# Three feature blocks per tile at the change of token halves, token states reloaded in chunks of the contraction, and the mask conversion on GpSimd

## The chip, the cores and the metric

The kernel runs on one core of a Trainium2 chip. The metric is the device time of one execution in microseconds (us); three runs of the kernel before took 2374.8 to 2379.33 us, with a median of 2378.59 us.

## What is computed

A decoder block with two token mixers over 2048 tokens of width 1024. One projection of the normalised input feeds both. Branch A is dense causal attention with low-rank queries and keys (8 heads). Branch B is sparse: an indexer scores all visible keys for each query, 256 of them are kept, and only these are attended. Each branch has a gate, and two sigmoid gates merge the branches. Cut to the core:

```python
h = rms_norm(x, norm_gain[l]); proj = h @ w_in[l]
(c_q, c_kv, k_pe, gate_a, q_b, k_b, v_b, gate_b, q_i, k_i, w_i, m_a, m_b) = jnp.split(proj, offsets, axis=-1)
# indexer of branch B, for a block of 128 queries
rel = jax.nn.relu(jnp.einsum('bqhd,bsd->bqhs', q_i, k_i))
score = jnp.where(causal, jnp.einsum('bqhs,bqh->bqs', rel, w_i), -jnp.inf)
_, sel = lax.top_k(score, 256)
# after the two attentions o_a and o_b
merged = (jax.nn.sigmoid(m_a + b_merge[l, 0]) * ((o_a * jax.nn.silu(gate_a)) @ w_branch_mla[l])
          + jax.nn.sigmoid(m_b + b_merge[l, 1]) * ((o_b * jax.nn.silu(gate_b)) @ w_branch_dsa[l]))
x = x + merged @ w_out[l]
```

## The kernel before, in words

Matrix products that need float32 accuracy are split into a high and a low part and made of three products (`mm3`, lines 111 to 115). The kernel has four stages. The first (to about 345 us) normalises and transposes the tokens and projects them to the small pieces (`project_tokens`). The second (345 to about 1090 us, `project_features`) is the one that the change touches. The third holds the two attentions (to about 1900 us), the last the merge and the output projection.

**Feature blocks.** The gates are 24 columns of 128 features (`c`), computed for 4 groups of 512 tokens. SBUF holds the transposed token states of two groups at a time, `hT[0]` and `hT[1]`, each as a high and a low tile of 128 x 8 x 512 float32 (2.1 MB each). After the first stage these hold the second half of the tokens; the states of the first half were written to DRAM, one tensor `d_h[t]` per 128 tokens (line 228), and come back with `load_h` (lines 335 to 338): four DMAs of 128 tokens for each of the two tiles, 512 KB each. A block (`feat`, line 340) is one column for one group: 24 matmuls of 512 columns, 3 for each of 8 chunks of the contraction. `FEATURES` (line 1175) is the order of the blocks: mostly column by column, both groups in turn. At the change of halves the order is by group: the last two columns of the second half for group 0, then for group 1, then `load_h` has brought the first half, and the first two columns follow for group 0 and for group 1. `load_h(g)` is called after column 23 of group g (line 1109).

**Weights.** A column's weights take one of three buffers (`preload`, line 1082). The next column's load starts when the last block that uses the buffer is done. In the first pass a column is loaded from the input and split on GpSimd (lines 236 to 238, then 108 and 109); in the second pass the split weights come back from DRAM (`load_split`, line 1097).

**Beside the blocks.** Between groups of six feature matmuls ("slots") the same stage works off other lanes. The indexer (`index_pair`, `scores`) handles query tiles in pairs: a matmul per head and 512 keys into `z` (line 387, three PSUM banks), a Relu on ScalarE into `zr` (line 389, six buffers), and a multiply-add on VectorE into the score tile `sc` (line 392; the first head is a scaled copy on ScalarE, line 398). Score tiles have two buffers, so pair n+2 takes the buffer of pair n. The search (`search`, line 405) of pair n runs while pair n+1 is scored: five Sign passes on ScalarE (line 439) with small steps on VectorE, then scans on VectorE (MAX8 and MATCH_REPLACE8, lines 468 and 473). At its end the scores become a 0-or-large mask: a Relu with a bias on ScalarE, line 476, from `sc` to `bias` (one buffer), stored to DRAM by line 477. There are 7 pairs, so 14 conversions, of 384 to 2048 columns. The other lane (`prepare`, line 528) makes the queries and keys of branch A, with its normalisation on GpSimd (lines 88, 569 to 575).

**Order of work.** The order on TensorE is the program's own. On the other engines and the DMA queue of SyncE the framework orders the instructions by a simulated timeline; each engine then runs its own queue in that order, and a waiting instruction holds up all that stand behind it.

Of the kernel before, what the change touches and what calls it, by code (L numbers as in the profile page):

```python
# [9 lines left out]
F32 = mybir.dt.float32  # L10
# [4 lines left out]
AF = mybir.ActivationFunctionType  # L15
OP = mybir.AluOpType
# [4 lines left out]
P = 128  # L21
S = 2048
D = 1024
NT = S // P
NG = S // 512
KC = D // P
H = 8
NEG = -1.0e30
SELECTED = -4.0e30
# [38 lines left out]
def bcast(ap, n):  # L68
    return bass.AP(tensor=ap.tensor, offset=ap.offset, ap=[[0, P], [1, n]])


class Block:
# [55 lines left out]
    def setup(self):  # L128
        nc = self.nc
        cp = self.pool(self.ctx, "consts")  # L130
        self.dp = self.pool(self.ctx, "spill", space=DRAM)
        self.cp = cp
        self.front = ExitStack()
        self.back = ExitStack()
        bk = self.pool(self.front, "front")
        fr = self.pool(self.back, "back", side="right")
        self.gains = fr.tile([P, N_GAIN], F32, name="gains")
        self.bm = bk.tile([P, 16], F32, name="bm")
        self.guess = fr.tile([P, len(PAIRS), 2, 4], F32, name="guess")
        pos = fr.tile([P, NT], I32, name="pos")  # L140
        self.ident = cp.tile([P, P], F32, name="ident")
        self.identr = fr.tile([P, P], F32R, name="identr")
        self.identb = cp.tile([P, P], BF, name="identb")
        self.negb = cp.tile([P, P], BF, name="negb")
        self.shift = fr.tile([P, 1], F32, name="shift")
        self.tri = fr.tile([P, P], F32, name="tri")
        self.trib = cp.tile([P, P], BF, name="trib")
        self.ones = cp.tile([P, 64], F32, name="ones")
        self.iota8 = fr.tile([P, 8], F32, name="iota8")
        self.bad = cp.tile([P, 1], F32, name="bad")  # L150
        self.sel = fr.tile([P, 1], F32, name="sel")
        self.half = fr.tile([P, 1], F32, name="half")
        nc.vector.memset(self.half, -0.5)
        nc.vector.memset(self.ones, 1.0)
        nc.vector.memset(self.bad, 0.0)
        nc.vector.memset(self.sel, SELECTED)
        d = fr.tile([P, P], I32, name="diff")
        nc.gpsimd.iota(d, pattern=[[1, P]], base=0, channel_multiplier=-1)
        nc.vector.tensor_scalar(self.ident, d, 0.0, None, op0=OP.is_equal)
        nc.vector.tensor_scalar(self.identr, d, 0.0, None, op0=OP.is_equal)  # L160
        nc.vector.tensor_scalar(self.identb, d, 0.0, None, op0=OP.is_equal)
        nc.vector.tensor_scalar(self.negb, d, 0.0, -1.0, op0=OP.is_equal, op1=OP.mult)
        nc.vector.memset(self.shift, -SELECTED / 2)
        nc.vector.tensor_scalar(self.tri, d, 0.0, NEG, op0=OP.is_gt, op1=OP.mult)
        nc.vector.tensor_scalar(self.trib, d, 0.0, NEG, op0=OP.is_gt, op1=OP.mult)
        i8 = fr.tile([P, 8], I32, name="i8")
        nc.gpsimd.iota(i8, pattern=[[1, 8]], base=0, channel_multiplier=0)
        nc.vector.tensor_copy(self.iota8, i8)
        self.pos = pos
        self.cos = fr.tile([P, NT, 16], F32, name="cos")  # L170
        self.sin = fr.tile([P, NT, 16], F32, name="sin")
        self.hT = [[bk.tile([P, KC, 512], F32R, name="hT%d%s" % (g, s)) for s in "hl"] for g in range(2)]
        self.w_i = fr.tile([P, NT, H], F32, name="w_i")
        self.kpe = fr.tile([P, NT, 33], F32, name="kpe")
        self.kT = fr.tile([P, S], F32R, name="kT")
# [30 lines left out]
    def hidden(self, tok, t):  # L206
        nc = self.nc
        x = tok.tile([P, D], F32, name="x", tag="x", bufs=X_BUFS)
        nc.sync.dma_start(x, self.a["x"][t * P:(t + 1) * P, :])
        if t == 0:  # L210
            nc.sync.dma_start(self.gnorm, bcast(self.a["norm_gain"], D))
        junk = tok.tile([P, D], BF, name="xj", tag="xj")
        ssq = tok.tile([P, 1], F32, name="xs", tag="xs", bufs=2)
        nc.scalar.activation(junk, x, AF.Square, accum_out=ssq)
        rstd = self.rsqrt(tok, ssq, 1, 1.0 / D, "x")
        nc.vector.scalar_tensor_tensor(x, x, rstd, self.gnorm, op0=OP.mult, op1=OP.mult)
        yield
        i, sl = t % 8, slice(t % 4 * P, t % 4 * P + P)
        hi, lo = (m[:, :, sl] for m in self.hT[i // 4])
        for b in range(2):  # L220
            ps = self.pp.tile([P, 4, P], F32, name="tr", tag="tr", bufs=3)
            for k in range(4):
                kc = 4 * b + k
                nc.tensor.transpose(ps[:, k], x[:, kc * P:(kc + 1) * P], self.ident)
            self.split(nc.scalar, hi[:, 4 * b:4 * b + 4], lo[:, 4 * b:4 * b + 4], ps, eng_lo=nc.vector)
        if t < 8:
            for s, m in enumerate((hi, lo)):
                self.move(self.d_h[t][:, s], m)

    def load_w(self, pool, src, n, name, bufs, engines, stage=None):  # L230
        nc = self.nc
# [101 lines left out]


    def load_h(self, g):
        for i in range(4):
            for s in range(2):
                self.move(self.hT[g][s][:, :, i * P:(i + 1) * P], self.d_h[4 * g + i][:, s])

    def feat(self, ev, hf, g, c, w):  # L340
        nc = self.nc
# [63 lines left out]
    def search(self, ip, n, ts, scs):  # L405
        nc, v = self.nc, self.nc.vector
# [19 lines left out]
        nt, d = cur[:, :, 0:1], cur[:, :, 1:2]  # L426
# [30 lines left out]
        for i, (t, sc) in enumerate(zip(ts, scs)):  # L457
            W = sc.shape[1]
            m8 = ip.tile([P, S], U8, name="m8", tag="m8")[:, :W]
            v.tensor_scalar(m8, sc, th[:, i, 0:1], None, op0=OP.is_gt, op1=OP.add, accum_out=th[:, i, 1:2])  # L460
            yield
            v.copy_predicated(sc, m8, self.sel.to_broadcast([P, W]))
            yield
            for r in range(2):
                v8 = ip.tile([P, 8], F32, name="v8", tag="v8", bufs=2)
                pen = ip.tile([P, 8], F32, name="pen", tag="pen", bufs=2)
                need = ip.tile([P, 1], F32, name="need", tag="need", bufs=2)
                v.max(v8, sc)
                v.tensor_scalar(need, th[:, i, 1:2], -1.0, float(TOPK - 8 * r), op0=OP.mult, op1=OP.add)
                v.tensor_scalar(pen, self.iota8, need, 3.0e38, op0=OP.is_ge, op1=OP.mult)  # L470
                v.tensor_tensor(v8, v8, pen, op=OP.add)
                yield
                v.match_replace(sc, v8, sc, SELECTED)
                yield
            bias = ip.tile([P, S], BF, name="bias", tag="bias", bufs=1)[:, :W]
            nc.scalar.activation(bias, sc, AF.Relu, bias=self.shift)
            nc.sync.dma_start(self.d_m[t][:, :W], bias)
        v.tensor_scalar(th[:, :, 2:3], th[:, :, 1:2], -1.0, TARGET, op0=OP.mult, op1=OP.add)
        v.tensor_tensor(th[:, :, 2:3], th[:, :, 2:3], th[:, :, 2:3], op=OP.mult)
# [447 lines left out]
    def run(self):  # L927
        nc, a = self.nc, self.a
        self.setup()
        self.d_w = [self.dram([P, 2, KC, P], F32, "d_w%d" % m) for m in range(24)]  # L930
        self.d_h = [self.dram([P, 2, KC, P], F32, "d_h%d" % t) for t in range(NT // 2)]
        self.d_qi = [self.dram([P, H, 32], F32, "d_qi%d" % t) for t in range(NT)]
        self.d_c = [self.dram([P, 2, 3, P], F32, "d_c%d" % t) for t in range(NT)]
        self.d_qb = [self.dram([P, H, P], F32, "d_qb%d" % t) for t in range(NT)]
# [177 lines left out]
    def project_features(self, fp, ip, stream):  # L1112
# [23 lines left out]
        slots = 8 * (48 - TAIL)  # L1136
        period = (PREPARE_SPAN * slots - 16) / (NT + 0.5)
        lanes = [[index(), 0, 2 * 14 + 8 * 38, INDEX_FIRST, INDEX_SPAN * slots], [search(), 0, SEARCH_RATE * slots, 0, slots]]
        lanes += [[prepare(s), 0, (4 + PREPARE_GAP) * NT, 16 + period * s / 2, 16 + period * (s / 2 + NT)] for s in range(2)]
        for slot in range(1, slots + 1):  # L1140
# [34 lines left out]
def feature_order():  # L1175
    order = []
    for half in range(2):
        pairs = [(c,) for c in range(24)]
        pairs = pairs[:22] + [(22, 23)] if half == 0 else [(0, 1)] + pairs[2:]
        order += [(half, g, 24 * half + c) for p in pairs for g in range(2) for c in p]  # L1180
    return order


FEATURES = feature_order()


# [68 lines left out]
```

## Time and profile before

| | |
|---|---|
| median of three runs | 2378.59 us (2374.8 to 2379.33) |
| the profiled execution | 2380.04 us, with a span of 2378.1 us |
| mean granted TensorE clock | 0.986 of full speed |
| busy: PE, DVE, POOL, ACT | 95%, 59%, 50%, 42% of the span |
| HBM read and written | 184.2 MB and 139.3 MB |

PE is TensorE, DVE VectorE, ACT ScalarE, POOL GpSimd, SP SyncE (SPq its DMA queue). A row "A <- B: t, n" says that engine A sat idle t us in n places until B released it. In a timeline row the first number is the start in us from the span's start, the second the duration; brackets hold the idle time ahead of it and what ended it. PEclk is the granted clock; 1.00 is 2.4 GHz and the lower level is 1.2 GHz.

### The profile page before, as it was taken

How to read it: one execution, taken by the hardware profiler on the slowest of the kernel's cores; microseconds unless marked ns; L12 is line 12 of the kernel's file. 1: busy time of each engine (PE TensorE's matmuls, PEld its weight loads, DVE VectorE, ACT ScalarE, POOL GpSimd, SP SyncE). 2: the span in 40 equal slices, each digit the busy share in tenths (PEclk: the TensorE clock that was granted, in tenths of full speed). 3: DMA queues.
4: the chain of work that ended last, by engine and by line, in shares of the span. 5: the costliest groups of instructions: out<-in, count | busy, mean ns of one | idle time of the engine just before them, and what ended most of it. 6: DMA issues, size and time to landing. Idle time of an engine off the chain costs nothing. (4 is left out here: it accounts for less than half of the span.)

```text
span 2378.1 us, 37994 instructions
## 1 busy us (share of the span) xinstructions
PE 2267.0 (95%) x12882; PEld 1757.5 (74%) x12882; DVE 1414.3 (59%) x3296; ACT 996.4 (42%) x2002; POOL 1194.4 (50%) x1541
## 2 busy tenths in 40 slices
PE   6999989999998999999999999999999999999999
PEld 6999988777776878886565655655655557888888
DVE  6453525588686787756766676677778664222222
ACT  5342325666656668532434434434434443101110
POOL 5876958766653433412444434334855446433331
PEclk9999999999999999999999999999999999999999
DMA  9441355665659656667433421220313003444442
GB/s 306 142 146 53 117 164 173 226 214 184 230 179 268 210 155 192 200 203 220 126 100 104 125 63 45 77 75 28 114 48 92 24 15 119 145 135 134 126 125 84
DMA packets 298100, 326.12 MB, mean 137 GB/s; under 512 B 23408, under 2 KB 228592, under 8 KB 297776
## 3 DMA queue, kind: packets, MB, share of 16 engines
q1 hardware_dynamic: 297392, 323.56, 43.5%
q8 instruction: 101, 1.65, 0.3%
q14 instruction: 95, 0.78, 0.1%
q10 hardware_dynamic: 512, 0.13, 0.0%
HBM read 184.20 MB, written 139.26 MB: 136 GB/s over the span
## 5 line engine op out<-in xcount | busy, mean ns | idle before, releaser
L672 ACT ACTIVATE pt<-st 128x512 f32<-128x512 f32 (+3 forms) x640 | 340.3, 534 | 434.7 <-PE st L646 392.1
L679 POOL TENSOR_TENSOR acc<-acc,pt 128x512 f32<-128x512 f32 (+3 forms) x288 | 327.3, 1137 | 362.8 <-ACT pt L672 352.0
L392 DVE SCALAR_TENSOR_TENSOR sc<-zr,w_i,sc 128x512 f32<-128x512 f32 (+3 forms) x266 | 218.9, 826 | 109.7 <-ACT zr L389 105.4
L646 PE MATMUL st<-Q,K 96*128 96x512 f32 (+3 forms) x960 | 265.1, 383 | 0.5 <-ACT ev L352 0.5
L607 DVE CUSTOM_DVE_ANT_0 mj<-ap,mask 128x512 bf16<-128x512 f32 (+2 forms) x320 | 193.7, 605 | 102.8 <-PE ap L600 94.2
L604 DVE TENSOR_REDUCE mx<-ap 128x1 f32<-128x512 f32 (+2 forms) x320 | 185.2, 604 | 115.0 <-PE ap L600 66.0
L679 DVE TENSOR_TENSOR acc<-acc,pt 128x512 f32<-128x512 f32 (+3 forms) x288 | 218.6, 759 | 51.3 <-ACT pt L672 46.1
L646 PEld LDWEIGHTS st<-Q,K 96*128 96x128 f32 (+1 forms) x960 | 163.1, 191 | 72.5 <-issue 49.8
L389 ACT ACTIVATE zr<-z 128x512 f32<-128x512 f32 (+3 forms) x304 | 163.0, 545 | 93.6 <-PE z L387 89.1
L113 PE MATMUL acc<-hT1h,wfh 128*128 128x512 f32 x384 | 157.4, 410 | 8.0 <-DMA hT1h<-d_h 7.1
L113 PE MATMUL acc<-hT0h,wfh 128*128 128x512 f32 x384 | 155.0, 404 | 1.4 <-DMA hT0h<-d_h 1.2
L114 PE MATMUL acc<-hT1l,wfh 128*128 128x512 f32 x384 | 152.8, 398 | 1.4 <-DMA d_f<-ev 1.4
L115 PE MATMUL acc<-hT1h,wfl 128*128 128x512 f32 x384 | 152.7, 398 | 0.0
L114 PE MATMUL acc<-hT0l,wfh 128*128 128x512 f32 x384 | 151.2, 394 | 1.1 <-DMA hT0l<-d_h 1.1
L115 PE MATMUL acc<-hT0h,wfl 128*128 128x512 f32 x384 | 151.2, 394 | 0.0
L686 PE MATMUL o<-pt,Vb 128*64 128x512 f32 (+3 forms) x640 | 135.3, 544 | 0.0
L686 PE MATMUL o<-pt,V 128*64 128x512 f32 (+3 forms) x640 | 135.1, 543 | 0.0
L646 PE MATMUL st<-Q,Kd 128*128 128x512 f32 (+3 forms) x320 | 132.9, 416 | 0.0
L106 ACT ACTIVATE mh<-sg 128x256 fp32r<-128x256 f32 x64 | 26.7, 417 | 249.5 <-POOL sg L909 249.4
L907 DVE TENSOR_TENSOR sg<-br,sg 128x256 f32<-128x256 f32 x128 | 53.3, 423 | 129.9 <-PE br L115 68.0
L387 PE MATMUL z<-kT,iqT 128*128 128x512 f32 (+3 forms) x304 | 111.1, 369 | 14.5 <-ACT zr L389 14.4
L600 PE MATMUL ap<-Kd,Q 128*128 128x512 f32 (+2 forms) x320 | 115.0, 375 | 3.5 <-DVE mx L607 3.4
(283 smaller groups left out, 5974.9 us busy)
## 6 DMA issues: line engine op xcount, KB each, us to landing
d_f<-ev SPq DMA_DIRECT2D x96, 256.0 KB
sg<-d_f SPq DMA_DIRECT2D x128, 128.0 KB
wst<-in_w_f SPq DMA_DIRECT2D x96, 128.0 KB
d_w<-wfh SPq DMA_DIRECT2D x24, 512.0 KB
d_w<-wfl SPq DMA_DIRECT2D x24, 512.0 KB
d_q<-phl SPq DMA_DIRECT2D x32, 384.0 KB
d_k<-phl SPq DMA_DIRECT2D x32, 384.0 KB
wfh<-d_w SPq DMA_DIRECT2D x24, 512.0 KB
```

The costliest lines, as they stand in the source:

```text
L113: mm(ps, lhi, rhi, start=start, stop=False)
L114: mm(ps, lhi, rlo, start=False, stop=False)
L115: mm(ps, llo, rhi, start=False, stop=stop)
L389: nc.scalar.activation(r[:, :n], z[:, :n], AF.Relu)
L392: nc.vector.scalar_tensor_tensor(sc[:, k0:k0 + n], r[:, :n], ws, sc[:, k0:k0 + n], op0=OP.mult, op1=OP.add)
L600: nc.tensor.matmul(ps[:, :n], q[:, i * P:(i + 1) * P], k(b)[:, :n], start=True, stop=not diag)
L604: nc.vector.tensor_reduce(mx[:, b:b + 1], ps[:, :n], axis=AX, op=OP.max)
L607: nc.vector.tensor_tensor_reduce(out=junk[:, :n], in0=ps[:, :n], in1=mask[i][:, 512 * b:512 * b + n], scale=1.0, scalar=-3.0e38, op0=OP.su ...
L646: nc.tensor.matmul(banks[hh][:, cols], l, r, start=start and n == 0, stop=stop and n == len(seq) - 1)
L672: nc.scalar.activation(pt[:, n0:], ps[:, n0:], AF.Exp, scale=u["scale"])
L679: eng.tensor_tensor(acc[:, n0:], acc[:, n0:], pt[:, n0:], op=OP.add)
L686: self.nc.tensor.matmul(u["o"][64 * hh:64 * hh + 64, n0:], u["v"](hh, j), pts[hh][:, n0:], start=(j == 0), stop=(j == u["nk"] - 1))
```

## The change

It has three parts. At the change of halves three columns, not two, are done for group 0 before group 1, on both sides of the change. The token states of the first half are kept in one DRAM tensor per group, laid out like the SBUF tile, and come back in four DMAs of two contraction chunks (512 tokens wide) for each tile, still 512 KB each. The mask conversion is a `tensor_scalar` (add, then max with 0) on GpSimd, and the constant tile that held the bias goes.

```diff
-        self.shift = fr.tile([P, 1], F32, name="shift")
-        nc.vector.memset(self.shift, -SELECTED / 2)
...
         if t < 8:
             for s, m in enumerate((hi, lo)):
-                self.move(self.d_h[t][:, s], m)
+                self.move(self.d_h[t // 4][:, s, :, sl], m)
...
     def load_h(self, g):
-        for i in range(4):
+        for k in range(0, KC, 2):
             for s in range(2):
-                self.move(self.hT[g][s][:, :, i * P:(i + 1) * P], self.d_h[4 * g + i][:, s])
+                self.move(self.hT[g][s][:, k:k + 2], self.d_h[g][:, s, k:k + 2])
...
-            nc.scalar.activation(bias, sc, AF.Relu, bias=self.shift)
+            nc.gpsimd.tensor_scalar(bias, sc, -SELECTED / 2, 0.0, op0=OP.add, op1=OP.max)
             nc.sync.dma_start(self.d_m[t][:, :W], bias)
...
-        self.d_h = [self.dram([P, 2, KC, P], F32, "d_h%d" % t) for t in range(NT // 2)]
+        self.d_h = [self.dram([P, 2, KC, 512], F32, "d_h%d" % g) for g in range(2)]
...
-        pairs = pairs[:22] + [(22, 23)] if half == 0 else [(0, 1)] + pairs[2:]
+        pairs = pairs[:21] + [(21, 22, 23)] if half == 0 else [(0, 1, 2)] + pairs[3:]
```

## Rows read from the trace of the kernel before

**Rows 1.** The page: busy time, share and instructions of each engine.

```profile
PE 2267.0 (95%) x12882; PEld 1757.5 (74%) x12882; DVE 1414.3 (59%) x3296; ACT 996.4 (42%) x2002; POOL 1194.4 (50%) x1541
```

**Rows 2.** Waits of PE over the whole span: us in total, times, longest.

```profile
PE z L387 <- ACT zr L389: 14.4, 8, 3.4
...
PE acc L113 <- DMA hT1h<-d_h: 7.1, 1, 7.1
...
PE acc L114 <- DMA d_f<-ev: 1.4, 1, 1.4
...
PE acc L113 <- DMA hT0h<-d_h: 1.2, 1, 1.2
PE acc L114 <- DMA hT0l<-d_h: 1.1, 1, 1.1
```

**Rows 3.** Windows, long: length, busy PE, PEld, DVE, ACT, POOL, PEclk, DMA, GB/s.

```profile
690.00:780.00 90.00, 74.72 (x336) 61.53 (x336) 56.60 (x125) 55.91 (x106) 29.46 (x30) 0.91 0.82 249
780.00:1085.00 305.00, 301.46 (x1428) 249.71 (x1427) 219.58 (x474) 184.28 (x339) 104.40 (x104) 0.99 0.62 192
```

**Rows 4.** Timeline of PE at the change of halves.

```profile
727.95 0.28 PE L387 MATMUL z<-kT,iqT 128*128 128x256 f32 x1
...
731.33 0.39 PE L115 MATMUL acc<-hT0h,wfl 128*128 128x512 f32 x1
...
746.70 0.39 PE L387 MATMUL z<-kT,iqT 128*128 128x512 f32 x1
754.24 0.76 PE L113 MATMUL acc<-hT1h,wfh 128*128 128x512 f32 x1 [7.15 <-DMA hT1h<-d_h]
...
761.01 0.40 PE L115 MATMUL acc<-hT1h,wfl 128*128 128x512 f32 x1
```

**Rows 5.** Timeline of the SP queue: first issue of each of the two reloads.

```profile
713.41 0.37 SPq L121 DMA_DIRECT2D hT0l<-d_h  x1
...
733.52 0.81 SPq L121 DMA_DIRECT2D hT1h<-d_h  x1
```

**Rows 6.** DMA issues in 713:731, and the window in which the second reload lands.

```profile
hT0l<-d_h SPq DMA_DIRECT2D x4, 512.0 KB
```

```profile
749.00:755.00 6.00, 0.76 (x1) 0.29 (x1) 4.64 (x10) 1.54 (x4) 5.68 (x5) 0.63 1.08 296
```

**Rows 7.** What the mask conversion waits for, and two of the 14 in ACT's timeline.

```profile
  DVE sc L473: 23.8, 10
```

```profile
517.11 2.00 ACT L476 ACTIVATE bias<-sc,shift 128x2048 bf16<-128x2048 f32 x1 [4.95 <-DVE sc L473]
...
887.76 1.57 ACT L476 ACTIVATE bias<-sc,shift 128x1536 bf16<-128x1536 f32 x1 [6.87 <-DVE sc L473]
```

**Rows 8.** Timeline of PE: three waits for `z` right behind conversions.

```profile
519.65 0.80 PE L387 MATMUL z<-kT,iqT 128*128 128x512 f32 x1 [3.37 <-ACT zr L389]
...
691.54 0.33 PE L387 MATMUL z<-kT,iqT 128*128 128x128 f32 x1 [1.53 <-ACT zr L389]
...
889.88 0.50 PE L387 MATMUL z<-kT,iqT 128*128 128x512 f32 x1 [3.33 <-ACT zr L389]
```

**Rows 9.** Windows of 10 us around two of them.

```profile
505.00:515.00 10.00, 10.00 (x47) 8.21 (x46) 10.00 (x18) 5.40 (x10) 10.00 (x13) 1.00 0.28 90
515.00:525.00 10.00, 6.63 (x21) 5.15 (x20) 9.44 (x17) 5.37 (x8) 5.77 (x6) 0.67 0.96 347
885.00:895.00 10.00, 6.67 (x23) 5.00 (x22) 10.00 (x18) 6.83 (x11) 2.47 (x4) 0.83 0.46 167
895.00:905.00 10.00, 10.00 (x46) 8.27 (x45) 7.69 (x16) 7.11 (x16) 6.98 (x7) 1.00 0.79 232
```

**Rows 10.** POOL: a one-input operation of 512 columns, and a wait in its timeline.

```profile
L677 POOL TENSOR_SCALAR acc<-pt x64: 618/621/632, 1092.7 to 1950.3; 128x512 f32<-128x512 f32 x64
```

```profile
896.85 0.68 POOL L88 TENSOR_SCALAR rs_p<-pss 128x8 f32<-128x8 f32 x1 [9.30 <-DVE pss L565]
```

**Rows 11.** ACT's first write into the reused score tile, and POOL's split of column 23.

```profile
529.01 0.72 ACT L398 ACTIVATE sc<-zr,w_i 128x512 f32<-128x512 f32 x1
```

```profile
684.74 0.67 POOL L108 TENSOR_SCALAR wfh<-wst 128x256 fp32r<-128x256 f32 x1 [4.31 <-DMA wst<-in_w_f]
```

**Rows 12.** The multiply-add of the scores on DVE: ns min, median, max.

```profile
L392 DVE SCALAR_TENSOR_TENSOR sc<-zr,w_i,sc x266: 334/750/2159, 360.9 to 1008.5; 128x512 f32<-128x512 f32 x100, 128x384 f32<-128x384 f32 x15, 128x256 f32<-128x256 f32 x10, 128x128 f32<-128x128 f32 x8
```

## The prediction, made before the changed kernel was run

> **What bounds the kernel now.** I read the page first: PE is busy 2267.0 of 2378.1 us [rows 1], so the kernel goes as fast as PE is fed, and only PE's 111 us of idle time, and the time it runs at its lower clock, can be won without removing products. The change removes no product. Next I read the list of PE's waits. Two families touch the change [rows 2]: 14.4 us of waiting for a `z` bank that ACT has not emptied, and 7.1 + 1.4 + 1.2 + 1.1 = 10.8 us of waiting for reloaded token states (the 1.4 is put down to a store, but the product reads hT1's low part and stands right behind the 7.1). Then the long windows, to see where this falls: 15.3 us are idle between 690 and 780 at a clock of 0.91, but only 3.5 in the 305 us behind it [rows 3]. Last the timelines, because a stall costs more than its idle time: after one, PE runs some products at half clock.
>
> **Part 1, the change of halves.** Undisturbed, a product of 512 columns starts every 0.23 us, one of 256 every 0.12 us (half of it is my estimate). The first reload makes the third product behind the `z` at 727.95 start at 731.33 [rows 4]; undisturbed it would be 727.95 + 0.12 + 2 x 0.23 = 728.53. Loss 2.8 us. In the second, 13 products start from 746.70 up to 761.01; at 0.23 they take 3.0 us, they took 14.3. Loss 11.3 us, though the waits are only 7.1 + 1.4: the rest is the low clock. Together **14.1 us** is all that part 1 can win.
>
> What must be true for that? The first reload is issued at 713.41 and needed at 727.95, 14.5 us of cover by two blocks, 7.3 us each [rows 4, 5]. It moves 8 x 512 KB = 4.2 MB; at the 296 GB/s of a window full of such traffic that is 14.2 us [rows 6], so it just misses. With three blocks the cover is about 21.8 us. The second reload is wanted from 727.95, but SP issues it only at 733.52, 5.6 us later, with the first reload's weights and stores ahead of it; PE comes for it at 746.9, after 18.9 us, of which 2.8 are the first stall, and gets it at 754.2. So it lands 26.3 us after it could have been issued, with 16.1 us of work as cover. Three blocks give 24.1 us at 8 us each. Pessimistically (nothing gets faster) 2.2 us of stall remain, some 4 us with the clock. But the 26.3 us include queueing behind the first reload, whose last piece had only just landed; with a block more between the two reloads its 14.2 us are over before the second begins: 5.6 us of issue delay, 3.5 us for one column's weights (1.05 MB at 296 GB/s) and 14.2 us make 23.3 us. And the pieces are now chunks of the contraction: a block's first six products need only the first chunk pair, the last pair is needed some 5 us later, whereas each token piece was needed by the first product. The new pieces are also longer runs in both memories; I give no gain for that, the cover suffices without it. So 10 to 14 us, and I take **-13 us**.
>
> What the move costs: the eight stores of each layout in the first stage are the same in number and bytes, and I take nothing for them; the SBUF side keeps its 512-byte runs. A store is issued with x loads behind it on SP's queue, so bounds are 0 and +1 us. Column 23's weights are now wanted two blocks after their buffer is free instead of three, and each of columns 24 to 27 two blocks ahead instead of three or four. Column 23 is split on POOL: its last piece starts at 684.74 [rows 11] and ends about 1.5 us later. The new order reaches column 23 for group 0 two blocks ahead of 713.41 [rows 5]; with a stall among them [rows 8] that is 691 to 699. Cover at least 5 us; if a conversion stands ahead of the piece in POOL's queue (the one in front of 691.54), it comes at about 693 to 694, and the last chunk pair is read some 5 us into the block. Bounds 0 and +3 us, taken as 0. The second-pass weights need no POOL, 3.5 us of transfer against 15 us of cover.
>
> **Part 2, the conversion.** On ACT it costs more than its time: ACT stands still for 23.8 us in 10 places until the last scan on DVE is done [rows 7], and everything behind it waits too, the Relu that empties `z` among it. The three waits in [rows 8] stand right behind conversions: at 517.11 ACT had been idle 4.95 us and then worked 2.00; at 887.76 it was 6.87 and 1.57 [rows 7]. Their price by the windows: 21 products where the window before has 47 is 26/47 of 10 us, 5.5 us; 23 against 46 in the window after is 5.0 us [rows 9]. With 1.5 us for the small one, **12.0 us**. The other waits for ACT in that family come behind Sign passes of the search, which stay.
>
> What the conversion costs on POOL: 14 of them, 17,024 columns together. A one-input operation of 512 columns takes 0.62 us there [rows 10], 1.2 ns a column, so some 21 us, 2.5 us for the longest. Cover: POOL is busy 104 of the last 305 us [rows 3], and at the conversion of 887.76 it sat idle for 9.30 us up to 896.85 [rows 10]. The waiting moves with it: POOL now stands until the scan is done, and behind it stand a weight split or the normalisation of `prepare`, which is asked for 17 slots, some 30 us, later. What is late next: DVE's own scans hold up the multiply-adds, but six `zr` buffers lie between them and PE. ACT's first write into the reused score tile waits for the conversions of two pairs back; the tightest is at 529.01 [rows 11], and POOL would end the second conversion at about 526 to 527, so 2 us of cover are left; without them ACT would stall there for the difference. Bounds for the whole part: all 12 us won, or none of it, since the framework orders four queues anew and a Sign pass can stand where the conversion stood. I take **-10 us**, near the upper end, because the idle row of POOL at the very place is the nearest one.
>
> **Sum.** 2380.04 (span 2378.1 plus 1.9 around it) - 13 - 10 = 2357.0 us. The profiled execution stands 1.45 us above the median shown, so against that I predict 2356 us, 1.0% less.
>
> **A rule against the change.** While POOL works, the multiply-add on DVE takes up to 2.16 us instead of its median 0.75 [rows 12], and in the windows where searches end DVE is already busy 10.0 and 9.4 of 10 us [rows 9]. The Trainium skill (GPSIMD Engine Reference, Specifications and Engine selection) says that GpSimd shares its SBUF interface with VectorE and contends with VectorE instructions that have two SBUF inputs, and advises VectorE for elementwise work, though one-input operations are near line rate; the spread of that row agrees with the contention. By it alone the second part would cost, not gain; it is the last rival below.
>
> **Rivals.** *Only the reload pays.* The search still stops ACT at its Sign passes, and the queues are ordered anew, so waits for `z` come back elsewhere for the same sum. For it: ACT's waits are between two engines that both run near a limit here. Against: three stalls stand directly at the conversions. Time: 2378.6 - 13 = 2366 us.
> *Weights take the place of tokens.* With three buffers and three columns per group, each column has two blocks of cover in place of four; a late split of column 23 and a weight load behind a reload cost 3 us idle each, 5 with the clock, as in the windows above. Time: 2356 + 10 = 2366 us. Against: 3.5 us of transfer each.
> *No change.* One part wins and the other loses about as much: 2378 us.
> *Slower: contention at the end of each search.* The place is DVE between the last scans and the next multiply-adds. During a conversion of some 1.5 us on average (21 us in 14) a multiply-add takes 1.4 us longer, and the following small steps too; if DVE falls more than six `zr` buffers behind, PE stops, and a stall of 1.3 us idle with its low clock costs about 2.6. It decides if it happens at nearly every conversion: 14 x 2.6 = 36 us less the 23 gained gives 2391 us. Against it: PE did not stop at most of the 14 places while ACT was stopped too.
>
> **How the numbers follow.** A difference under 0.2%, 4.8 us, is about what a measurement of this kernel can't tell from none. Forecast with both parts, 2346 (all of both, and the ordering kind) to 2361: 0.60. Only the reload, 2361 to 2370: 0.19. Late weights, same times: 0.08. No change: 0.06. Slower: 0.07. The range 2346 to 2370 holds the first three, 0.87, less what may fall beyond either end. Faster 0.87, same 0.06, slower 0.07.
>
> **What would show it.** Right: no wait of PE for a reload above 1 us, and a clock near 1.00 between 690 and 780; no ACT idle time in front of a conversion, and POOL idle instead until the same scan; the wait for `z` down from 14.4 to 4 to 6 us. Wrong: a wait of PE on weights around columns 23 to 27; a scaled copy on ACT waiting for POOL; longer multiply-adds on DVE with waits for `z` at the same places; a wait for `z` as large as before, now behind Sign passes.

## The result and the profile after

The changed kernel takes 2404.88 us (median of four runs, 2398.43 to 2407.56) against 2378.11 of the kernel before in the same series (2374.80 to 2379.33): ratio 1.0102, 95% interval 1.008 to 1.0124. It is slower by 1%. The forecast was 2356 us, 1% faster, with 2346 to 2370 as its range. Of the two parts one did what was forecast: no reload of token states is left in PE's list of waits, and PE is better fed at the change of halves. The other lost more than the first won.

The profiled execution took 2402.92 us, its span 2400.9. The page's busy row; DVE is busy 21.6 us and POOL 62.3 us longer than in [rows 1], ACT 19.3 us shorter:

```profile
PE 2277.5 (95%) x12882; PEld 1764.5 (73%) x12882; DVE 1435.9 (60%) x3295; ACT 977.1 (41%) x1988; POOL 1256.7 (52%) x1555
```

PE's waits over the whole span (us in total, times, longest), to be held against [rows 2]:

```profile
PE tr L581 <- DVE phl L109: 16.2, 2, 9.2
...
PE z L385 <- ACT zr L387: 11.0, 8, 3.0
PE tr L581 <- ACT iqT L376: 7.3, 2, 6.6
...
PE acc L113 <- ACT pqk L558: 6.0, 3, 3.3
PE tr L118 <- DVE phl L109: 3.9, 1, 3.9
```

The wait for `z` fell from 14.4 to 11.0 only. In place of the reload stand waits of up to 9.2 us for work of `prepare` (`phl`, `pqk`) and of the index (`iqT`), which DVE and ACT deliver late. The long windows show where the time went (length, busy PE with its products, PEld, DVE, ACT, POOL, granted clock, DMA share, GB/s):

```profile
345.00:690.00 345.00, 324.31 (x1494) 266.42 (x1495) 245.30 (x439) 209.91 (x405) 260.04 (x313) 0.98 0.58 194
690.00:780.00 90.00, 78.28 (x367) 65.08 (x366) 61.78 (x130) 53.67 (x107) 46.91 (x40) 0.94 0.75 260
780.00:1085.00 305.00, 289.23 (x1332) 239.64 (x1331) 223.91 (x450) 173.63 (x328) 132.58 (x106) 0.97 0.55 176
```

The first of these windows in the kernel before:

```profile
345.00:690.00 345.00, 329.73 (x1526) 271.94 (x1525) 244.81 (x456) 217.19 (x412) 244.07 (x309) 0.98 0.61 201
```

Between 690 and 780 PE starts 367 products in place of the 336 of [rows 3]. It starts 32 fewer in the window ahead and 96 fewer in the one behind (1332 in place of 1428). At the forecast's 0.23 us each, an estimate since some products are shorter, 128 products lost and 31 gained make 22 us; the span grew by 22.8. POOL is busy 132.6 us in the last window, not 104.4.

**The conversion on POOL.** First the line's own row (count, min, median, max in ns), then some of the 14 in the list of groups by shape (busy us, mean ns, idle before):

```profile
L474 POOL TENSOR_SCALAR bias<-sc x14: 1501/4310/7100, 519.7 to 1078.5; 128x2048 bf16<-128x2048 f32 x1, 128x384 bf16<-128x384 f32 x1, 128x1920 bf16<-128x1920 f32 x1, 128x512 bf16<-128x512 f32 x1
```

```profile
L474 POOL TENSOR_SCALAR bias<-sc 128x2048 bf16<-128x2048 f32 x1 | 7.1, 7100 | 3.6 <-DVE sc L471 3.6
...
L474 POOL TENSOR_SCALAR bias<-sc 128x1152 bf16<-128x1152 f32 x1 | 4.1, 4092 | 6.2 <-DMA d_f<-ev 6.2
...
L474 POOL TENSOR_SCALAR bias<-sc 128x512 bf16<-128x512 f32 x1 | 1.9, 1927 | 0.1
```

That is 3.5 ns a column, where the forecast had 1.2 from [rows 10]; the 14 sum to 61.9 us, not 21, and the longest takes 7.1 us, not 2.5. The one of 1152 columns ran at 1078.53, when DVE had nothing to do, and took 3.55 ns a column all the same: the price is the instruction's own.

**What it does to DVE.** The timeline of POOL, then DVE, at the first conversion:

```profile
519.68 7.10 POOL L474 TENSOR_SCALAR bias<-sc 128x2048 bf16<-128x2048 f32 x1 [3.64 <-DVE sc L471]
...
520.31 0.54 DVE L471 MATCH_REPLACE8 sc<-v,sc 128x384 f32<-128x384 f32 x1
520.77 3.44 DVE L480 TENSOR_TENSOR bad<-bad,th 128x1 f32<-128x1 f32 x1
524.12 0.74 DVE L390 SCALAR_TENSOR_TENSOR sc<-zr,w_i,sc 128x512 f32<-128x512 f32 x1
524.79 2.02 DVE L563 TENSOR_SCALAR pss<-pss,kpe 128x8 f32<-128x8 f32 x1
```

The same steps in the kernel before:

```profile
517.79 0.54 DVE L473 MATCH_REPLACE8 sc<-v,sc 128x384 f32<-128x384 f32 x1
518.25 0.14 DVE L482 TENSOR_TENSOR bad<-bad,th 128x1 f32<-128x1 f32 x1
518.32 0.74 DVE L392 SCALAR_TENSOR_TENSOR sc<-zr,w_i,sc 128x512 f32<-128x512 f32 x1
518.98 0.22 DVE L565 TENSOR_SCALAR pss<-pss,kpe 128x8 f32<-128x8 f32 x1
```

A scan goes on undisturbed beside POOL (0.54 us both times), but an operation on a single column, with two inputs, takes 3.44 us in place of 0.14, and a small one with a value per partition 2.02 in place of 0.22. DVE works in order, so the multiply-adds of the scores stand behind them. The Trainium skill (SBUF — State Buffer, "Who interferes with whom") says that a VectorE instruction with two SBUF inputs contends with a GpSimd instruction that reads SBUF. By the 3.44 us against 0.14 this trace agrees. The same section says of VectorE's modes with two ports that whoever comes first holds the shared ports for the whole instruction, and that the other is blocked, not slowed. The one-column operation was not held so long: it ended at 524.21, while the conversion ran until 526.78.

**How it reaches PE.** Two of the stalls, first ACT and PE after the conversion just shown, then DVE and PE after the one of 1792 columns that started at 701.55 (the last number in brackets is the idle time before, with what ended it):

```profile
530.83 0.52 ACT L412 ACTIVATE junk<-sc 128x384 bf16<-128x384 f32 x1 [10.34 <-DVE sc L390]
...
531.98 1.09 PE L581 MATMUL tr<-ident,pqk 128*96 128x128 f32 x4 [6.57 <-ACT iqT L376]
...
701.77 5.02 DVE L390 SCALAR_TENSOR_TENSOR sc<-zr,w_i,sc 128x512 f32<-128x512 f32 x2
...
710.10 0.68 DVE L109 TENSOR_TENSOR phl<-tr,phl 96x512 fp32r<-96x512 f32 x1
710.83 1.09 PE L581 MATMUL tr<-ident,pqk 128*96 128x128 f32 x4 [9.16 <-DVE phl L109]
```

At the first, ACT no longer stands at the conversion; it stands 10.34 us at the next search's first statistics pass, which needs the last multiply-add of the scores, and `iqT` is queued behind that pass. At the second, two multiply-adds that take 0.75 us each by their median take 5.02 us together, `phl` comes behind them, and PE stops for 9.16 us. The longest single multiply-add is now 4.66 us; in [rows 12] it was 2.16.

### The profile page after: what moved, and what is told of

Its sections match the earlier page's. It is cut to its first block, busy times and chain, and to the rows that moved or that the text cites. A ratio compares the mean times of both kernels' runs of the same rounds, so it can differ in the third digit from the quotient of the medians.

```text
span 2400.9 us, 38042 instructions
## 1 busy us (share of the span) xinstructions
PE 2277.5 (95%) x12882; PEld 1764.5 (73%) x12882; DVE 1435.9 (60%) x3295; ACT 977.1 (41%) x1988; POOL 1256.7 (52%) x1555
## 4 chain that ended last, share of the span: by engine, by line
PE 54%; DVE 13%; DMA 6%; issue 5%; ACT 5%; POOL 4%; SPq 1%; DVEq 0%; ACTq 0%; POOLq 0%
PE st L644 17%; PE o L684 11%; PE ap L598 5%; DVE sc L390 4%; PE acc L113 3%; PE acc L114 3%; PE acc L115 3%; ACT junk L437 2%; DMA out_dram<-mx 2%; PE br L113 2%; PE br L115 2%; PE br L114 2%; PE ou L115 2%; PE ou L114 2%; PE ou L113 2%
## 5 line engine op out<-in xcount | busy, mean ns | idle before, releaser
L390 DVE SCALAR_TENSOR_TENSOR sc<-zr,w_i,sc 128x512 f32<-128x512 f32 (+3 forms) x266 | 225.1, 849 | 99.2 <-ACT zr L387 94.8
```

Source lines behind the costliest of these rows:

```text
L390: nc.vector.scalar_tensor_tensor(sc[:, k0:k0 + n], r[:, :n], ws, sc[:, k0:k0 + n], op0=OP.mult, op1=OP.add)
```

## The experiments

Two theories to begin with. **T**: only the conversion on GpSimd was mispriced, and it makes the whole loss. **R1**: the new order of blocks and queues makes the new stalls, whatever engine converts.

**1. The reload's part alone** (the change, with the conversion as before):

```diff
-            nc.gpsimd.tensor_scalar(bias, sc, -SELECTED / 2, 0.0, op0=OP.add, op1=OP.max)
+            nc.scalar.activation(bias, sc, AF.Relu, bias=self.shift)
```

> The change with its conversion put back on ACT: three blocks per tile and the reload by chunks alone. T (the conversion on GpSimd was mispriced and makes the whole loss, the reload pays as forecast): 2362 to 2369 us, against 2378 of before, and no wait of PE on the token states in its list. R1 (the new order of the blocks and queues makes the new stalls of PE, whatever engine converts): 2378 us or more, with PE's waits on the weights' and the index's values (7 to 9 us each) still there.

Measured: 2362.34 us against 2381.08 of before on that chip, ratio 0.9916 (0.9894 to 0.9939). In its list of waits no wait for a reloaded token state is left. T holds, R1 falls. The windows:

```profile
345.00:690.00 345.00, 326.88 (x1526) 269.54 (x1524) 244.50 (x458) 217.99 (x414) 244.21 (x310) 0.99 0.61 200
690.00:780.00 90.00, 85.54 (x404) 72.02 (x405) 62.73 (x133) 61.52 (x118) 33.92 (x33) 0.96 0.79 272
780.00:1085.00 305.00, 301.01 (x1424) 246.97 (x1425) 218.96 (x487) 180.80 (x333) 103.35 (x103) 0.99 0.63 197
```

Sixty-eight products more than in [rows 3] between 690 and 780, with nearly the same number as before on either side (1526 and 1428 there): the gain sits at the change of halves.

**2. The conversion's part alone** (the kernel before, with line 476 in the change's form):

> The kernel before with only the conversion moved to GpSimd. T: 2410 to 2420 us, the 14 conversions 55 to 65 us in all on POOL, and PE waits of 7 us or more behind late first passes of the next search. R1: 2366 to 2382 us, since the order of the blocks is that of before.

Measured: 2412.24 us, ratio 1.0128 (1.0111 to 1.0145). By itself the second part costs some 30 us. In the change it costs 36 to 44 us by the ratios (1.0102 against 0.9916 of the reload alone, and against 0.9949 in its second series, under 6); the intervals leave open whether the two parts simply add. Its 14 conversions take as long as in the change (1502 to 7100 ns), and PE's waits for `phl` (8.7 us the longest) and `iqT` (6.6) are there in the old order of blocks too.

**3. The conversion on DVE:**

```diff
-            nc.gpsimd.tensor_scalar(bias, sc, -SELECTED / 2, 0.0, op0=OP.add, op1=OP.max)
+            nc.vector.tensor_scalar(bias, sc, -SELECTED, None, op0=OP.add)
```

> The change with the conversion as one subtraction on DVE (the chosen values become 0, the others 4e30 instead of 2e30, so the mask is the same). T: it costs DVE what its other passes over f32 cost, some 14 to 20 us in all and nobody waits behind it on POOL: 2358 to 2372 us. If DVE at the end of a search is itself what the next search and PE wait for, 2372 to 2390 us. R1: above 2395 us, since the order stays.

Measured: 2375.19 us, ratio 0.9974 (0.9958 to 0.9989). The 14 conversions cost DVE 12.7 us, on an engine that the search itself waits for; the result lies in the second of the three ranges, 13 us above the reload alone on the same chip.

**4. What makes a column cost 3.5 ns?** Two forms by turns:

```diff
-            nc.gpsimd.tensor_scalar(bias, sc, -SELECTED / 2, 0.0, op0=OP.add, op1=OP.max)
+            if n % 2:
+                nc.gpsimd.tensor_scalar(bias, sc, 1.0, -SELECTED, op0=OP.mult, op1=OP.add)
+            else:
+                nc.gpsimd.tensor_scalar(sc, sc, -SELECTED / 2, 0.0, op0=OP.add, op1=OP.max)
+                nc.scalar.activation(bias, sc, AF.Copy)
```

> The change with two other forms of the conversion by turns. Odd pairs: multiply by 1 and add on GpSimd, from f32 to bf16. Even pairs: add and maximum on GpSimd from f32 to f32 in place, and then a copy to bf16 on ACT. It is meant to tell which feature makes a column cost 3 to 4 ns instead of the 1.2 ns of the forecast. If the bf16 output does: even pairs 1.2 ns, odd pairs 3 to 4 ns a column. If the operations do (the maximum): even pairs 3 to 4 ns, odd 1.2. If the place and its neighbours on DVE do: both 3 to 4 ns, the one that runs alone at the end less. Time of the whole: 2390 to 2415 us by any of the three.

```profile
L477 POOL TENSOR_SCALAR sc<-sc 128x1536 f32<-128x1536 f32 x1 | 5.4, 5393 | 2.4 <-DVE sc L471 2.4
...
L475 POOL TENSOR_SCALAR bias<-sc 128x1920 bf16<-128x1920 f32 x1 | 1.8, 1794 | 1.1 <-DVE sc L471 1.1
```

Add and maximum cost 3.5 ns a column with an f32 output as well; multiply and add cost 0.93 ns with the bf16 output, at the same places in the schedule. So it is the pair of operations, not the type and not the place. The whole took 2382.52 us (a single run).

**5. Which operation?** Three more forms by turns:

```diff
+            if n % 3 == 0:
+                nc.gpsimd.tensor_scalar(bias, sc, -SELECTED, None, op0=OP.add)
+            elif n % 3 == 1:
+                nc.gpsimd.tensor_scalar(bias, sc, SELECTED / 2, -SELECTED / 2, op0=OP.max, op1=OP.add)
+            else:
+                nc.gpsimd.tensor_scalar(bias, sc, SELECTED / 2, -NEG, op0=OP.is_gt, op1=OP.mult)
```

> The change with three more forms of the conversion on GpSimd, by turns: pairs 0, 3, 6 one addition alone; pairs 1, 4 a maximum first and then an addition; pairs 2, 5 a comparison and then a multiplication. If an operation of maximum is what is slow on GpSimd: pairs 1 and 4 cost 3 to 4 ns a column, the others about 1 ns. If an addition in the first place is slow: pairs 0, 3, 6 cost 3 to 4 ns and pairs 1 and 4 about 1 ns. The comparison can fall on either side. Time of the whole: 2360 to 2395 us.

```profile
L475 POOL TENSOR_SCALAR bias<-sc 128x2048 bf16<-128x2048 f32 x1 | 5.4, 5384 | 3.6 <-DVE sc L471 3.6
...
L477 POOL TENSOR_SCALAR bias<-sc 128x1536 bf16<-128x1536 f32 x1 | 5.4, 5384 | 2.4 <-DVE sc L471 2.4
...
L479 POOL TENSOR_SCALAR bias<-sc 128x1408 bf16<-128x1408 f32 x1 | 5.0, 4966 | 2.1 <-DVE sc L471 2.1
```

Neither of my two guesses: one addition alone costs 2.6 to 3.2 ns a column, maximum and addition 3.5 to 3.8, comparison and multiplication 3.5 to 4.2. Of the five forms tried, only multiply followed by add is near 1 ns. Why, these runs don't show. Time 2402.11 us (a single run); all of its conversions are slow ones.

**6. The forecast's own price.** All conversions as multiply and subtract:

```diff
-            nc.gpsimd.tensor_scalar(bias, sc, -SELECTED / 2, 0.0, op0=OP.add, op1=OP.max)
+            nc.gpsimd.tensor_scalar(bias, sc, 1.0, -SELECTED, op0=OP.mult, op1=OP.add)
```

> The change with every conversion on GpSimd in the form of the odd pairs of the run before: multiply by 1 and subtract, no maximum; there it took 1.05 ns a column, close to the forecast's price. T (only the price of the operation was wrong, the rest of the forecast holds): 2350 to 2362 us, below the 2362 of the reload alone, with PE's wait for z down to 4 to 8 us. R2 (a conversion on GpSimd gains nothing even at the forecast's price, since ACT then waits at its next pass): 2362 to 2370 us, no better than the reload alone.

Measured: 2369.00 us, ratio 0.995 (0.9927 to 0.9972). The 14 sum to 18.4 us. That lies in the range of R2, not in that of T, which goes by the forecast. That run stood on another chip than the reload alone, so both were run again together:

> The reload's part alone once more, on one chip with the two others: 2360 to 2370 us.

> The change with its conversions on GpSimd as multiply and subtract once more, on one chip with the reload alone. If the forecast's second part holds at its own price: 8 us or more below the reload alone. If ACT only waits at the search's next pass in place of the conversion (R2): within 3 us of the reload alone, or above it.

Measured: the reload alone 2369.07 us, ratio 0.9949 (0.993 to 0.9968); with the quick conversion on GpSimd 2366.63 us, 0.9926 (0.9911 to 0.9941). The difference is 2.4 us, and the intervals overlap; in the first pair it stood the other way round. So no gain of the second part is shown, even at its own price. The waits tell why. First PE's over the span and ACT's between 505 and 1090, of the reload alone:

```profile
PE z L387 <- ACT zr L389: 14.1, 7, 3.4
...
ACT bias L476 <- DVE sc L473: 23.4, 8, 6.9
...
ACT junk L439 <- DVE cur L429: 6.1, 4, 2.4
```

The same with the quick conversion on GpSimd:

```profile
PE tr L581 <- DVE phl L109: 6.4, 2, 5.6
PE tr L581 <- ACT iqT L376: 6.4, 3, 3.6
PE z L385 <- ACT zr L387: 5.9, 5, 2.3
...
ACT junk L412 <- DVE sc L390: 15.5, 5, 7.4
...
ACT junk L437 <- DVE cur L427: 10.4, 5, 3.5
```

The wait for `z` does fall to the 4 to 6 us that the forecast named, 8.2 us less. But ACT, freed from waiting at the conversion, waits at the next passes of the search, whose input is made by the same DVE (15.5 us at line 412, where the reload alone has 1.7, and 10.4 in place of 6.1 at line 437), and `iqT` and `phl` are queued behind those: PE's waits for these two at line 581, 6.4 us each, are 4.7 and 3.4 us longer than in the reload alone.

**7. Later conversions on ACT.** The reload's part, both conversions of a pair issued three steps of the search later:

```diff
+            for _ in range(3 * i):
+                yield
+            if i:
+                for t, sc in zip(ts, scs):
+                    bias = ip.tile([P, S], BF, name="bias", tag="bias", bufs=1)[:, :sc.shape[1]]
+                    nc.scalar.activation(bias, sc, AF.Relu, bias=self.shift)
```

> The reload's part with the conversions still on ACT, but both conversions of a pair issued three steps of the search after its last scan was issued, so that ACT does not reach them before the scan has ended. If ACT's 23 us of waiting at the conversions is what part 2 of the forecast was to win: 2350 to 2357 us, 5 to 12 below the reload alone. If the wait goes on to the next pass in the queue: within 4 us of the reload alone.

Measured: 2367.69 us, ratio 0.9936 (0.9919 to 0.9953), as the reload alone. But ACT still waits 23.6 us in 9 places at the conversions: the delay did not bring them behind DVE's scan, so this run decides nothing.

**8. Which half of the reload's part?** Three blocks per tile, with the token states still stored and reloaded by tokens:

> Three blocks per tile at the change of halves, the token states still stored and reloaded by tokens, the conversion on ACT: half of the reload's part. The forecast's working: three blocks alone give the first reload 21.8 us of cover for 14.2 us, and the second 24.1 for 23.3, but each piece is needed by the first product of its block: 2362 to 2368 us, with 0 to 4 us of PE's waits for token states left. The rival, that the longer runs of the chunk layout are what pays: 2372 to 2380 us, with the waits near the 10.8 us of before.

Measured: 2371.92 us, ratio 0.996 (0.9941 to 0.9979), between the two ranges. Of PE's waits for reloaded states one is left:

```profile
PE acc L114 <- DMA hT1l<-d_h: 1.2, 1, 1.2
```

So the three blocks alone remove nearly all of the 10.8 us of waiting. What the chunks add is not shown: 0.996 overlaps the 0.9949 of one series of the reload alone in its interval and just misses the 0.9916 of the other (0.9939 at its upper end, on another chip).

**9. Why does a long conversion cost so much?** First, is it the form or the time that GpSimd is held? The quick form, issued three times at each place (55.5 us in all):

> The quick form of the conversion (multiply by 1 and subtract), issued three times in a row at each place, so that GpSimd is held about as long as by the change's form: some 55 us in all in place of 62. If it is the time that GpSimd is held that costs (its queue, and DVE's instructions that stretch beside it): 2385 to 2400 us. If the slow form does something else beside being long: 2355 to 2372 us.

Measured: 2401.91 us, ratio 1.0084 (1.0052 to 1.0116). That is 2 us above the first of the two ranges and 30 above the second: it is the time, and the quick form loses as much when GpSimd works on it about as long. That leaves two ways: **Q**, what stands behind the conversion in GpSimd's queue comes late; **D**, DVE is stopped. To tell them apart, GpSimd was held as long by an instruction that moves few bytes, with the conversion back on ACT:

```diff
             nc.scalar.activation(bias, sc, AF.Relu, bias=self.shift)
+            hold = ip.tile([P, 48], F32, name="hold", tag="hold", bufs=1)[:, :W // 48]
+            nc.gpsimd.tensor_scalar(hold, sc[:, :W // 48], 1.0e-31, 1.0, op0=OP.mult, op1=OP.add)
+            nc.gpsimd.tensor_tensor(hold, hold, self.half.to_broadcast([P, W // 48]), op=OP.pow)
```

> The reload's part with the conversion on ACT, and behind each conversion a power of one column in 48 on GpSimd, whose result is used nowhere: GpSimd is held from the same scan on for about as long as by the change's conversion (some 65 us in all), but reads and writes a 48th of the bytes. Two ways in which a long conversion can cost: Q, the queue (normalisation, weight splits and the search's own square root stand behind it on GpSimd): 2385 to 2402 us. D, DVE's instructions of two inputs or with a value per partition, which stretch while GpSimd works on whole tiles: 2360 to 2372 us, near the reload alone. If a power stretches them too, the trace shows DVE's smallest operations at 2 us or more beside it, and Q and D stay unseparated.

Measured: 2373.70 us, ratio 0.9962 (0.9945 to 0.9979), some 3 to 5 us above the reload alone beside it, and 2 us above D's range. POOL and DVE at the first place:

```profile
518.53 7.07 POOL L479 TENSOR_TENSOR hold<-hold,half 128x42 f32<-128x42 f32 x1
...
519.30 0.14 DVE L485 TENSOR_TENSOR bad<-bad,th 128x1 f32<-128x1 f32 x1
519.36 0.74 DVE L392 SCALAR_TENSOR_TENSOR sc<-zr,w_i,sc 128x512 f32<-128x512 f32 x1
520.03 0.22 DVE L568 TENSOR_SCALAR pss<-pss,kpe 128x8 f32<-128x8 f32 x1
```

POOL is held 7.07 us, and DVE's steps are as long as in the kernel before. The counterpart has the change's own instruction over the whole tile in that place, its result unused:

```diff
             nc.scalar.activation(bias, sc, AF.Relu, bias=self.shift)
+            hold = ip.tile([P, S], BF, name="hold", tag="hold", bufs=1)[:, :W]
+            nc.gpsimd.tensor_scalar(hold, sc, -SELECTED / 2, 0.0, op0=OP.add, op1=OP.max)
```

> The reload's part with the conversion on ACT, and behind each the change's own instruction on GpSimd over the whole tile (add and maximum, f32 to bf16), with its result used nowhere. It differs from the run with the power in the bytes read and written and in the operation, and holds GpSimd as long. D: 2388 to 2405 us, 20 or more above the run with the power, with the smallest operations of DVE at 1 us or more on average beside it. Q': near the run with the power, 2366 to 2378 us.

Measured: 2389.09 us, ratio 1.0055 (1.0033 to 1.0077): in D's range, though the run with the power, on another chip, is 15 us below it by the times and 22 by the ratios, not clearly the 20 expected. DVE's steps are stopped again:

```profile
521.40 7.10 POOL L478 TENSOR_SCALAR hold<-sc 128x2048 bf16<-128x2048 f32 x1 [1.75 <-DVE sc L473]
...
522.49 3.44 DVE L484 TENSOR_TENSOR bad<-bad,th 128x1 f32<-128x1 f32 x1
```

The same in the change's order of queues, a quick conversion with a power behind it:

```diff
             nc.gpsimd.tensor_scalar(bias, sc, 1.0, -SELECTED, op0=OP.mult, op1=OP.add)
+            hold = ip.tile([P, 32], F32, name="hold", tag="hold", bufs=1)[:, :W // 70]
+            nc.gpsimd.tensor_scalar(hold, sc[:, :W // 70], 1.0e-31, 1.0, op0=OP.mult, op1=OP.add)
+            nc.gpsimd.tensor_tensor(hold, hold, self.half.to_broadcast([P, W // 70]), op=OP.pow)
```

> The change with the quick conversion on GpSimd (multiply and subtract), and behind it a power of one column in 70 with an unused result, so that GpSimd is held at each place about as long as by the change's conversion, in the change's order of queues. D (DVE is stopped by the long instruction over whole tiles): 2366 to 2378 us, within 10 of the quick conversion alone. Q' (GpSimd held for long costs, once the conversion and its store are in its queue): 2390 to 2405 us.

Measured: 2377.69 us, ratio 0.9983 (0.9966 to 1.0001), at the upper end of D's range. Put together, by ratios, since the runs come from several chips (GpSimd held in all at the conversions' places; mean of DVE's one-column operation between 505 and 1090). The column "DVE put off" is worked out from the traces. For every instruction of DVE that ran beside one of these on GpSimd, I took the time from the end of DVE's instruction before it (or from its own start, where that is later) to its own end, and subtracted the median of the same instruction in the kernel before. The column is the sum.

| kernel | GpSimd held, us | one column on DVE, ns | DVE put off, us | ratio to before |
|---|---|---|---|---|
| reload alone, second series | 0 | 315 | 0 | 0.9949 |
| reload, power | 66.3 | 308 | 1.8 | 0.9962 |
| reload, whole tile, slow form | 62.7 | 1082 | 27.8 | 1.0055 |
| quick conversion, second series | 18.7 | 472 | 8.2 | 0.9926 |
| quick conversion, power | 68.3 | 352 | 9.0 | 0.9983 |
| quick conversion, thrice | 55.5 | 417 | 29.5 | 1.0084 |
| the change | 61.9 | 1082 | 28.7 | 1.0102 |

Holding GpSimd costs 0.0013 in the one order, which is within the intervals, and 0.0057 in the other (3 and 14 us of 2381; 0.0033, 8 us, against the first series of the quick conversion, 0.995, where the intervals overlap). DVE is put off about as long with the power as without it there, 9.0 and 8.2 us. Moving whole tiles in that time costs 0.0093 and 0.0119 more (22 and 28 us). So D is the larger part and Q the smaller, by differences that carry some 6 us of uncertainty each.

Three quick conversions stop the one-column operation less than one slow one, and still cost nearly as much. The column "DVE put off" shows why: there the stop falls on other instructions, the multiply-adds above all. At the first place of that run:

```profile
518.48 4.32 POOL L475 TENSOR_SCALAR bias<-sc 128x2048 bf16<-128x2048 f32 x2 [1.05 <-DVE sc L471]
...
519.56 0.82 DVE L481 TENSOR_TENSOR bad<-bad,th 128x1 f32<-128x1 f32 x1
...
523.20 2.43 DVE L390 SCALAR_TENSOR_TENSOR sc<-zr,w_i,sc 128x512 f32<-128x512 f32 x1
```

In all, whole tiles on GpSimd put DVE off by about half of the time that they take (0.41 to 0.55 of it over the runs with one form throughout), in the quick form as in the slow one, and the loss goes with that sum. The power puts it off by 1.8 us in 66. The power is also another operation, so that the bytes moved make the difference is likely, not shown by itself.

**The best version.** The reload alone (0.9916 and 0.9949) and the change with the quick conversion (0.995 and 0.9926) beat the kernel before and the changed one. Between them these runs show no difference.

## Why the prediction was wrong

**Part 1, the reload, taken at -13 us: right.** Measured alone -19 and -14 us by the medians of the two series. The first lies above the 14.1 us that the working allowed at most (its interval is 14.5 to 25 us, that of the second 8 to 17), so the mechanism is shown and the size within some 6 us. The cover was argued to suffice with the blocks alone, and it did, but for 1.2 us of waiting.

**Part 2, the price: the step that failed.** "A one-input operation of 512 columns takes 0.62 us there, 1.2 ns a column, so some 21 us, 2.5 us for the longest." The row was that of a multiply and add; the change's form is an add and a maximum, and it cost 3.5 ns a column or more, 61.9 us in all and 7.1 us for the longest. By the ratios that price alone is worth 36 to 42 us (1.0102 of the change against 0.995 and 0.9926 with the quick form), most of the 49 us between forecast and result. The nearest row by engine, size and number of inputs was not the nearest by operation, and I gave no bound for that. With the right price the rest of the working would have told of trouble: it left 2 us of cover at 529.01, and it had conversions of 2.5 us at most ahead of POOL's other work.

**Part 2, the gain, taken at -10 us: wrong too.** At its own price the second part gives -2 us in one pair of runs and +7 in the other, where the two stood on different chips. Of the 14.1 us of `z` waits 8.2 do go, as forecast; the step "all 12 us won, or none of it" named the rest itself, and the lower end was the one that came. I put the value near the upper end because POOL was idle at the place. What decides is not whether POOL has room but who feeds ACT next: the search's next pass, by the same late DVE.

**The rivals.** "Slower: contention at the end of each search", at 0.07, is the one that came: the place, DVE between the last scans and the next multiply-adds, was right, and its price came near, 2391 us forecast, 2405 measured. But its way to PE was another: it had PE stop at `z` when the six buffers run out, and PE's wait for `z` fell, from 14.4 to 11.0 us. The stops came by ACT's statistics pass, `iqT` and `phl`, so the nearness of the price is in part luck. I sized its trigger by a conversion of 1.5 us on average, so it looked rare; at 4.4 us (61.9 in 14) it puts DVE off by 28.7 us in all, where the quick form does by 8.2. And what I set against it, that PE did not stop at most places while ACT was stopped, is no evidence for a stop of DVE. The rule cited from the Trainium skill (GPSIMD Engine Reference, "Engine selection") that one-input operations run near line rate on GpSimd holds here for multiply and add alone (about 1 ns a column), not for the forms with a single addition, a maximum or a comparison (2.6 to 4.2 ns).

**The signs.** Of what was to show the forecast wrong, "longer multiply-adds on DVE" came true (4.66 us), but the waits behind it were for `iqT` and `phl`, not for `z`. Of what was to show it right, the waits for the reload went and POOL stood idle in front of the conversions in ACT's place; the clock between 690 and 780 rose from 0.91 to 0.94 only (0.96 with the reload alone), and `z` stayed at 11.0 us.

## What to carry to other kernels

Price an instruction on GpSimd by a row of the same operations, not only of the same engine, size and number of inputs; where there is none, keep a bound several times higher, and prefer a form that the kernel already shows to be quick. Before moving whole-tile work onto GpSimd, look at what DVE does at that moment: here operations with two inputs, and a small one with a value per partition, stood still beside it, however few their columns, and everything queued behind them was late. And an engine freed from a wait at the head of its queue has won nothing if its next instruction waits for the same producer.

## What I had not expected of the hardware

- The price of a column on GpSimd depends on the operations: multiply and add about 1 ns, an addition alone 2.6 to 3.2, the pairs with a maximum or a comparison 3.5 to 4.2. For add and maximum the output type makes no difference.
- DVE's 128x1 operation took 3.44 us beside a whole-tile instruction of GpSimd, and 0.14 us beside a power of 7.07 us that also reads and writes SBUF, but few bytes: that GpSimd is busy is not what stops DVE. Work on whole tiles does, by about half of its time, in the quick form too. Even beside the whole tile DVE was let in once before its end (the multiply-add at 524.12 took its usual 0.74 us while the conversion ran until 526.8).
